# Modulation gathers inside the next step, and modulation rows behind the next step's weights

## The chip, the cores and the metric

The kernel runs on one core of one Trainium2 chip. The metric is the device time of one execution in microseconds (us), the median of several runs; lower is better. Engines are named as the profile names them: PE (TensorE, the matmuls), DVE (VectorE), ACT (ScalarE), POOL (GpSimd) and SP, whose queue issues the DMAs spoken of here.

## The reference, cut to what matters

Two layers of a trunk of width 1024 run over 640 tokens (512 of a sample, 128 of a prompt). Each layer is a feed-forward block (FFN1), a mixing block of attention and Fourier heads, and a second feed-forward block (FFN2). Nine modulation vectors of 1024 elements per layer and kind of token shift, scale and gate the three blocks; they come from a conditioning vector through the weight w_mod.

```python
def swiglu(h, w_gu, w_down):
    g, u = jnp.split(h @ w_gu, 2, axis=-1)
    return (jax.nn.silu(g) * u) @ w_down

    mod = jax.nn.silu(cvec) @ w_mod[l] + b_mod[l]
    sh1, sc1, gt1, sh2, sc2, gt2, sh3, sc3, gt3 = [m[:, None, :] for m in jnp.split(mod, N_MOD, -1)]
    f1 = swiglu(x * (1 + sc1) + sh1, w_ffn1_gu[l], w_ffn1_down[l])
    x = layer_norm(ALPHA * x + 0.5 * gt1 * f1, ln_g[l, 0], ln_b[l, 0])
    mo, new = token_mix(x * (1 + sc2) + sh2, ...)
    x = layer_norm(ALPHA * x + gt2 * mo, ln_g[l, 1], ln_b[l, 1])
    f2 = swiglu(x * (1 + sc3) + sh3, w_ffn2_gu[l], w_ffn2_down[l])
    x = layer_norm(ALPHA * x + 0.5 * gt3 * f2, ln_g[l, 2], ln_b[l, 2])
```

Inputs and weights are 32-bit floats. w_gu has 2 x 2816 columns, w_down 2816 rows.

## The kernel before

**Products.** Activations lie with the width on the partitions and the 640 tokens in two halves of 320 columns. Each 32-bit value is split in a high part (hi, ACT, L162) and the rest (lo, DVE, L167), so that a product of two values is three matmuls (L116 to L118), of 320 columns each.

**Weights.** A weight tile of 512 KB is a Unit. Its fetch (L146) loads it by SP's queue into a ring of four raw buffers; then ACT writes hi and DVE writes lo into rings of four, and the raw buffer is free again. A Pair (L184) loads two tiles at once and has a chain of sums on DVE between its raw buffers (L204 to L215); its matmuls are those of L121 to L123 (out of them pa, pb, pc, pd).

**A feed-forward block** has 22 tiles t of 128 hidden columns, in three parts of 8, 7 and 7. In FFN1 tiles t = 0 to 10 are plain: each is a step of a gate product g and an up product u, 96 matmuls in all, followed by silu and product (ACT L724, DVE L726) and the split of the result (L113). Tiles from 11 on are taken in pairs. After each part come eight down steps m = 0 to 7 (d, 48 matmuls in part 0), whose result DVE adds to the state xt with the gate (L985). In part 0 the down steps have DVE make the block sums for the pairs beside it (L751 to L757).

**Modulation.** A modulation vector is a group of eight rows of w_mod (each 128 x 1024). A row is a unit without hi and lo: it takes one raw buffer, and DVE multiplies it with the conditioning values into an accumulator of two halves (L368 for a group's first row, L370 for the other seven; two instructions for each row). After the eighth row a gather of four matmuls on PE (L380) adds over the partitions, ACT copies the result (L389), a turn of four transposes on PE (L395) puts it back on partitions, and DVE adds the bias (L400). There is one accumulator, so the first row of the next group waits for the gather of the last. FFN1 of each layer carries six groups (j = 2 to 7), FFN2 of layer 0 three, FFN2 of layer 1 one: 16 with a gather here.

**Order.** with_mods (L2002) puts rows behind the main steps: each main step adds its rate to a sum `due`, and for each whole one a row unit follows. The rates of FFN1 are 1.0 for t=0, 4.0 for t=1, 8/3 for the plain steps and 10/7; each down step of part 0 takes four. When a group's last row is placed, the list `late` gets the gather and the turn: the gather becomes a step of its own behind the next whole main step, and the turn one behind the step after that. The list `flat` of all units, in the order of the steps, is the order of loading, and so of SP's queue; prep_to loads and converts up to a step's units, and advance and fetch_ahead load and convert ahead as far as there is room in the rings (four raw buffers). A row unit that stands behind step t in the steps also stands ahead of the weights of step t+1 in that order. Within the steps the order of instructions on an engine is the scheduler's, which keeps to priorities of the program's order and to buffers.

Of the kernel before, what the change touches and what calls it, by code (L numbers as in the profile page):

```python
# [29 lines left out]
PARTS = (8, 7, 7)  # L30
MIDW = max(PARTS) * T
PLAIN = {1: 11, 2: 6}
MOD_RATE = {1: (1.0, 4.0, 8 / 3, 10 / 7), 2: (1.0, 3.0, 1.0, 8 / 6)}
BUSY = 2
T_BUFS = 9
E_BUFS = 6
# [23 lines left out]
def trunk_kernel(ctx: ExitStack, tc: tile.TileContext, a, y_prompt, y_sample, new_a_k, new_a_v, new_b_k, new_b_v):  # L60
# [171 lines left out]
        return Unit([(0, n, w[k0 * 128 : (k0 + nk) * 128, c0 : c0 + n].rearrange("(k p) c -> p k c", p=128))], nk, n)  # L232

    steps = []
    flat, index, ptr = [], {}, [0]

    def prep_to(n):
# [456 lines left out]
    def ffn_steps(l, which, gate_fn, pre=None):  # L694
# [150 lines left out]
        t = 0  # L845
        for pi, n in enumerate(PARTS):
            final = pi == len(PARTS) - 1
            for i in range(n):
                if t == 0:
                    u0, u1 = gu(0), gu(1)  # L850
                    u0[0].extra = True

                    def head(u0=u0, u1=u1):
                        if not pre:
                            new_mid()
                        with tc.manual_schedule() if pre else nullcontext():
                            if pre:
                                pre[0]()
                            accs = [Acc("g0", True), Acc("u0", False), Acc("g1", True)]
                            head_group([u0[0], u0[1], u1[0]], accs, pre and pre[1])  # L860
                        if pre:
                            new_mid()
                        finish(0, accs[0], accs[1])
                        loc["g1"] = accs[2]

                    steps.append(([u0[0], u0[1], u1[0]], head, bool(pre), 0.0 if pre else rates[0]))

                    def second(u1=u1):
                        pu = Acc("u1", False, bank)
                        for hf in range(2):  # L870
                            project(u1[1], pu.h[hf], hf)
                        finish(1, loc.pop("g1"), pu)
                        park(4)

                    step([u1[1]], second, rates[1])
                elif 1 < t < plain:
                    u = gu(t)

                    def body(u=u, i=i, t=t):
                        if i == 0:  # L880
                            new_mid()
                        pg, pu = Acc("g", True), Acc("u", False)
                        for hf in range(2):
                            project(u[0], pg.h[hf], hf)
                        for hf in range(2):
                            project(u[1], pu.h[hf], hf)
                        finish(i, pg, pu)
                        if t == 2:
                            park(4)
                        if which == 2:  # L890
                            for k in {3: (0, 1), 4: (2,), 5: (3,)}.get(t, ()):
                                block_sums(k)
                        if t == plain - 1:
                            block_third()

                    step(list(u), body, rates[2])
                elif t >= plain:
                    pair = Pair(cols(t * 128), cols(FFN + t * 128))
                    us = [pair, Sums(pair, "u"), Sums(pair, "g")]
                    loc[t] = us  # L900
                    pair.chained, pair.follows = i < n - 1, i > 0 and t > plain

                    def body(us=us, i=i, t=t, n=n):
                        if i == 0:
                            new_mid()
                        if i == 0 or t == plain:
                            loc["region"] = tc.manual_schedule(engines={ENG.PE, ENG.Activation, ENG.DVE})
                            loc["region"].__enter__()
                        seven(i, us, loc[t + 1] if i < n - 1 else None, t == FT - 1)
                        if i == n - 1:  # L910
                            loc.pop("region").__exit__(None, None, None)
                        if t == FT - 1:
                            unpark()

                    step(us, body)
                if i == n - 1 and not final:
                    last_gu = steps[-1]

                    def more(fn=last_gu[1]):
                        fn()  # L920
                        fetch(0)
                        fetch(1)

                    steps[-1] = (last_gu[0], more, *last_gu[2:])
                t += 1
# [9 lines left out]
            for m in range(KT - nskew):  # L935
                u = du(m)

                def body(u=u, m=m, n=n, pi=pi, final=final):
                    p = Acc("d", m % 2 == 0)
                    if final:  # L940
                        if m == 0:
                            ln.begin()
                        ln.pre(m)
                    for hf in range(2):
                        down_mm(u, p.h[hf], hf, n)
                    for hf in range(2):
                        if final:
                            ln.residual(m, hf, p.h[hf])
                        else:
                            plain_residual(xt[m], m, hf, p.h[hf], gate_fn())  # L950
                    if not final:
                        nc.sync.dma_start(out=parked[m], in_=xt.pop(m))
                        if m + 2 < KT:
                            fetch(m + 2)
                    if which == 1 and pi == 0 and m % 2 == 1:
                        block_sums(m // 2)

                step([u], body, 0.0 if final or m >= KT - BUSY + (which == 1) else rates[3])
# [1043 lines left out]
    def with_mods(build, mod_list):  # L2002
# [2 lines left out]
        main = steps[lo:]  # L2005
        del steps[lo:]
        groups = [mod_steps(*m) for m in mod_list]
        due, late = 0.0, []
        for s in main:
            steps.append(s)  # L2010
            while late:
                steps.append(([], late.pop(0), False, 0.0))
                if late:
                    break
            due += s[3]
            while groups and s[3] and due > 0.999:
                ms, gather, turn = groups[0]
                steps.append(ms.pop(0))
                due -= 1.0
                if not ms:  # L2020
                    groups.pop(0)
                    late += [gather, turn]
                    break
        assert not groups, len(groups)

    def fetch_late():
# [9 lines left out]
    for l in range(DEPTH):  # L2036
# [8 lines left out]
        with_mods(  # L2045
            lambda: ffn_steps(l, 2, gate_of(l, 8, True)), [(l, 8)] + ([(l + 1, 0), (l + 1, 1)] if l + 1 < DEPTH else [])
        )
    flat.extend(u for units, *_ in steps for u in units)
    index.update((id(u), i) for i, u in enumerate(flat))
    seen = 0  # L2050
    for units, fn, manual, _ in steps:
        seen += len(units)
        if not manual:
            prep_to(seen)
            if units and not getattr(units[0], "chained", False):
                advance()
            else:
                fetch_ahead()
# [66 lines left out]
```

## Time and profile before

| | |
|---|---|
| median of 3 runs | 2584.7 us (2583.87 to 2588.28) |
| the profiled execution | 2578.7 us |
| its span | 2576.9 us |
| granted PE clock, mean | 0.983 |
| PE busy | 96% of the span |
| DVE, ACT, POOL busy | 74%, 41%, 2% |
| DMA, read and written | 127 GB/s over the span |

[...] Idle time of an engine counts only where PE waits for it.

### The profile page before, as it was taken

To read this page: it belongs to the slowest core of one execution; us is meant where nothing else is said; L and a number is where in the kernel's file an instruction comes from. 1 tells how busy PE (TensorE), PEld (TensorE's weight loads), DVE (VectorE), ACT (ScalarE), POOL (GpSimd) and SP (SyncE) were. 2 spreads that over 40 slices of the span, in tenths; PEclk is the share of its full clock that TensorE was granted. 3 is DMA by queue.
4 is the path that set the end of the run, shared out by engine and by line. 5 is a ranking of instruction groups with operands and counts; after the bars stand their busy time and mean duration, and the time that the engine had idled before them with its cause. 6 is when DMAs were issued, how large, how long until landed. Compare 5 with 4: busy or idle time off the path is not lost. (4 is left out here: it accounts for less than half of the span.)

```text
span 2576.9 us, 41839 instructions
## 1 busy us (share of the span) xinstructions
PE 2467.0 (96%) x16759; PEld 2377.6 (92%) x16759; DVE 1916.2 (74%) x3266; ACT 1065.7 (41%) x1942; POOL 44.0 (2%) x42
## 2 busy tenths in 40 slices
PE   8889899999999999999998889999999999999998
PEld 6789899999879999999988889999998799999998
DVE  5568778776776896878784678787688678667577
ACT  3212324455675632424361123243666755323242
POOL 0000000001000000000000000000010000000000
PEclk9899999999999999999999899999999999999999
DMA  9556464423123445372444454624331225434332
GB/s 270 162 173 208 120 195 125 136 97 107 52 65 99 150 129 172 94 222 84 142 150 149 151 166 126 215 81 137 107 97 40 60 99 180 133 97 133 114 119 78
DMA packets 400560, 337.11 MB, mean 131 GB/s; under 512 B 13802, under 2 KB 352492, under 8 KB 399852
## 3 DMA queue, kind: packets, MB, share of 16 engines
q1 hardware_dynamic: 400364, 334.43, 42.4%
q8 instruction: 132, 2.16, 0.4%
q14 instruction: 64, 0.52, 0.1%
HBM read 286.93 MB, written 40.63 MB: 127 GB/s over the span
## 5 line engine op out<-in xcount | busy, mean ns | idle before, releaser
L162 ACT CAST hi<-raw 128x1024 fp32r<-128x1024 f32 (+5 forms) x382 | 388.0, 1018 | 805.5 <-PE pd L122 186.6
L167 DVE TENSOR_TENSOR lo<-raw,hi 128x1024 fp32r<-128x1024 f32 (+5 forms) x382 | 451.1, 1183 | 143.9 <-ACT hi L162 142.1
L116 PE MATMUL d<-midh,hi 128*128 128x320 f32 x1366 | 425.0, 312 | 14.2 <-ACT hi L162 14.2
L118 PE MATMUL d<-midh,lo 128*128 128x320 f32 x1366 | 423.6, 311 | 1.4 <-DVE lo L167 1.4
L117 PE MATMUL d<-midl,hi 128*128 128x320 f32 x1366 | 424.7, 311 | 0.1
L370 DVE SCALAR_TENSOR_TENSOR acc<-raw,csil,acc 128x1024 f32<-128x1024 f32 x224 | 277.7, 1277 | 7.4 <-DMA raw<-in_w_mod_dram 7.4
L116 PEld LDWEIGHTS d<-midh,hi 128*128 128x128 f32 x1366 | 258.1, 189 | 20.0 <-ACT hi L162 14.7
L117 PEld LDWEIGHTS d<-midl,hi 128*128 128x128 f32 x1366 | 258.4, 189 | 2.1 <-DVE midl L837 1.8
L118 PEld LDWEIGHTS d<-midh,lo 128*128 128x128 f32 x1366 | 257.9, 189 | 2.4 <-DVE lo L167 2.4
L116 PE MATMUL g<-hh,hi 128*128 128x320 f32 x480 | 154.4, 322 | 28.5 <-ACT hi L162 28.5
L118 PE MATMUL u<-hh,lo 128*128 128x320 f32 x544 | 168.2, 309 | 0.7 <-DVE lo L167 0.7
L116 PE MATMUL u<-hh,hi 128*128 128x320 f32 x544 | 168.3, 309 | 0.0
L117 PE MATMUL u<-hl,hi 128*128 128x320 f32 x544 | 168.3, 309 | 0.0
L118 PE MATMUL g<-hh,lo 128*128 128x320 f32 x480 | 153.8, 320 | 2.4 <-DVE lo L167 2.4
L117 PE MATMUL g<-hl,hi 128*128 128x320 f32 x480 | 153.5, 320 | 0.0
L985 DVE SCALAR_TENSOR_TENSOR xt<-d,gate,xt 128x320 f32<-128x320 f32 (+2 forms) x192 | 75.3, 433 | 91.3 <-PE d L118 91.1
L121 PE MATMUL pa<-hh,hi 128*128 128x320 f32 x432 | 134.4, 311 | 0.9 <-ACT up L797 0.7
L123 PE MATMUL pa<-hh,lo 128*128 128x320 f32 x432 | 133.6, 309 | 0.9 <-DVE lo L167 0.9
L122 PE MATMUL pa<-hl,hi 128*128 128x320 f32 x432 | 133.5, 309 | 0.0
L116 PEld LDWEIGHTS g<-hh,hi 128*128 128x128 f32 x480 | 94.6, 197 | 30.9 <-ACT hi L162 29.7
L118 PEld LDWEIGHTS u<-hh,lo 128*128 128x128 f32 x544 | 102.1, 188 | 1.0 <-DVE lo L167 1.0
L116 PEld LDWEIGHTS u<-hh,hi 128*128 128x128 f32 x544 | 102.1, 188 | 0.1
(608 smaller groups left out, 6353.1 us busy)
## 6 DMA issues: line engine op xcount, KB each, us to landing
raw<-in_w_ffn_gu_dram SPq DMA_DIRECT2D x176, 512.0 KB
raw<-in_w_mod_dram SPq DMA_DIRECT2D x128, 512.0 KB
raw<-in_w_ffn_down_dram SPq DMA_DIRECT2D x56, 448.0 KB
xt<-park SPq DMA_DIRECT2D x64, 320.0 KB
park<-xt SPq DMA_DIRECT2D x64, 320.0 KB
raw<-in_w_ffn_down_dram SPq DMA_DIRECT2D x36, 512.0 KB
raw<-in_w_in_dram SPq DMA_DIRECT2D x26, 512.0 KB
park<-trunk SPq DMA_DIRECT2D x32, 320.0 KB
```

What stands on the lines that cost most here:

```text
L116: nc.tensor.matmul(out, wh, xh, start=first, stop=False)
L117: nc.tensor.matmul(out, wh, xl, start=False, stop=False)
L118: nc.tensor.matmul(out, wl, xh, start=False, stop=last)
L121: nc.tensor.matmul(out, wh, xh, start=first, stop=False, skip_group_check=True)
L122: nc.tensor.matmul(out, wh, xl, start=False, stop=False, skip_group_check=True)
L123: nc.tensor.matmul(out, wl, xh, start=False, stop=last, skip_group_check=True)
L162: nc.scalar.copy(hi, self.raw.rearrange("p k n -> p (k n)"))
L167: nc.vector.tensor_sub(self.l, self.raw, self.h)
L370: nc.vector.scalar_tensor_tensor(acc[:, s, :], w, cs, acc[:, s, :], op0=ALU.mult, op1=ALU.add)
L985: nc.vector.scalar_tensor_tensor(x[:, s0:s1], ps[:, s0 - hf * HW : s1 - hf * HW], gate[:, m, s : s + 1], x[:, s0:s1], op0=ALU.mult, op1=AL ...
```

## The change

Three things are changed, all in the order of the work; no instruction is added or left out of what is computed.

The gather and the turn of a group no longer are steps. When the group's last row is placed, both are put on a list of hooks, and the next main steps call them from inside: a plain gate and up step calls one between the two halves of its up product and one after its end; a down step calls one after each half's product. The first gate and up steps and the pairs call none.

Row units no longer stand ahead of the next step's weights in the order of loading. They wait on a list, and follow the next units with a split; only a Pair has them ahead of it.

The rate of FFN1's plain steps is 3.0 where it was 8/3, and 0.0 in the last plain tile, t=10. Between t=2 and t=10 there are 24 rows either way.

```diff
--- before.py
+++ after.py
@@ -30,7 +30,7 @@
 PARTS = (8, 7, 7)
 MIDW = max(PARTS) * T
 PLAIN = {1: 11, 2: 6}
-MOD_RATE = {1: (1.0, 4.0, 8 / 3, 10 / 7), 2: (1.0, 3.0, 1.0, 8 / 6)}
+MOD_RATE = {1: (1.0, 4.0, 3.0, 10 / 7), 2: (1.0, 3.0, 1.0, 8 / 6)}
 BUSY = 2
 T_BUFS = 9
 E_BUFS = 6
@@ -232,6 +232,12 @@
         return Unit([(0, n, w[k0 * 128 : (k0 + nk) * 128, c0 : c0 + n].rearrange("(k p) c -> p k c", p=128))], nk, n)
 
     steps = []
+    hooks = []
+
+    def hook():
+        if hooks:
+            hooks.pop(0)()
+
     flat, index, ptr = [], {}, [0]
 
     def prep_to(n):
@@ -883,8 +889,11 @@
                         for hf in range(2):
                             project(u[0], pg.h[hf], hf)
                         for hf in range(2):
+                            if hf:
+                                hook()
                             project(u[1], pu.h[hf], hf)
                         finish(i, pg, pu)
+                        hook()
                         if t == 2:
                             park(4)
                         if which == 2:
@@ -893,7 +902,7 @@
                         if t == plain - 1:
                             block_third()
 
-                    step(list(u), body, rates[2])
+                    step(list(u), body, rates[2] if which == 2 or t < plain - 1 else 0.0)
                 elif t >= plain:
                     pair = Pair(cols(t * 128), cols(FFN + t * 128))
                     us = [pair, Sums(pair, "u"), Sums(pair, "g")]
@@ -943,6 +952,7 @@
                         ln.pre(m)
                     for hf in range(2):
                         down_mm(u, p.h[hf], hf, n)
+                        hook()
                     for hf in range(2):
                         if final:
                             ln.residual(m, hf, p.h[hf])
@@ -2005,22 +2015,25 @@
         main = steps[lo:]
         del steps[lo:]
         groups = [mod_steps(*m) for m in mod_list]
-        due, late = 0.0, []
+        due = 0.0
         for s in main:
             steps.append(s)
-            while late:
-                steps.append(([], late.pop(0), False, 0.0))
-                if late:
-                    break
             due += s[3]
             while groups and s[3] and due > 0.999:
                 ms, gather, turn = groups[0]
-                steps.append(ms.pop(0))
+                units, fn, *rest = ms.pop(0)
                 due -= 1.0
-                if not ms:
-                    groups.pop(0)
-                    late += [gather, turn]
-                    break
+                if ms:
+                    steps.append((units, fn, *rest))
+                    continue
+
+                def last(fn=fn, gather=gather, turn=turn):
+                    fn()
+                    hooks.extend([gather, turn])
+
+                steps.append((units, last, *rest))
+                groups.pop(0)
+                break
         assert not groups, len(groups)
 
     def fetch_late():
@@ -2045,13 +2058,18 @@
         with_mods(
             lambda: ffn_steps(l, 2, gate_of(l, 8, True)), [(l, 8)] + ([(l + 1, 0), (l + 1, 1)] if l + 1 < DEPTH else [])
         )
-    flat.extend(u for units, *_ in steps for u in units)
+    wait = []
+    for units, *_ in steps:
+        if units and not units[0].split:
+            wait += units
+        elif units:
+            flat.extend([*wait, *units] if isinstance(units[0], Pair) else [*units, *wait])
+            wait = []
     index.update((id(u), i) for i, u in enumerate(flat))
-    seen = 0
     for units, fn, manual, _ in steps:
-        seen += len(units)
+        if units and not manual:
+            prep_to(index[id(units[-1])] + 1)
         if not manual:
-            prep_to(seen)
             if units and not getattr(units[0], "chained", False):
                 advance()
             else:
```

The new listings number the lines from L372 on six higher (L368 is L374, L380 is L386) and those behind the down step's hook ten higher (L985 is L995).

**SP's queue, layer 0, around the weights of t=5.** Before; raw_878 and raw_884 are the weights of t=4, raw_1124 and raw_1130 those of t=5, raw_761 the last row of group 2, the four rows behind t=4 are the first of group 3, and the two cs loads belong to another table:

```order
L146 DMA raw_878<-in_w_ffn1_gu_dram 128x8x128
L146 DMA raw_884<-in_w_ffn1_gu_dram 128x8x128
L146 DMA raw_890<-in_w_mod_dram 128x1024
L146 DMA raw_894<-in_w_mod_dram 128x1024
L146 DMA raw_1003<-in_w_mod_dram 128x1024
L146 DMA raw_1007<-in_w_mod_dram 128x1024
L1920 DMA cs02_5286<-in_cache_b_k_dram 128x128
L1920 DMA cs03_5291<-in_cache_b_k_dram 128x128
L146 DMA raw_1124<-in_w_ffn1_gu_dram 128x8x128
L146 DMA raw_1130<-in_w_ffn1_gu_dram 128x8x128
```

After; raw_880 is a weight of t=4, raw_886 the last row of group 2, raw_890 and raw_894 are the weights of t=5, raw_898 to raw_1143 rows of group 3, and raw_1147 and raw_1153 the weights of t=6:

```order
L146 DMA raw_880<-in_w_ffn1_gu_dram 128x8x128
L146 DMA raw_886<-in_w_mod_dram 128x1024
L146 DMA raw_890<-in_w_ffn1_gu_dram 128x8x128
L146 DMA raw_894<-in_w_ffn1_gu_dram 128x8x128
L146 DMA raw_898<-in_w_mod_dram 128x1024
L146 DMA raw_1013<-in_w_mod_dram 128x1024
L146 DMA raw_1015<-in_w_mod_dram 128x1024
L146 DMA raw_1019<-in_w_mod_dram 128x1024
L146 DMA raw_1143<-in_w_mod_dram 128x1024
L146 DMA raw_1147<-in_w_ffn1_gu_dram 128x8x128
L146 DMA raw_1153<-in_w_ffn1_gu_dram 128x8x128
```

The weights of t=5 have moved from behind the first four rows of group 3 to ahead of all of them.

**DVE, layer 0, around the first row of group 3.** Before; acc0_2 and acc0_3 are the accumulator for groups 2 and 3, silu_1108 is t=4, and lo_1127 and lo_1133 belong to t=5:

```order
L726 TENSOR_TENSOR silu_1108<-silu_1108,u_0_1010 128x320
L726 TENSOR_TENSOR silu_1108<-silu_1108,u_1_1011 128x320
L368 TENSOR_SCALAR acc0_3_1121<-raw_890,csil_102 128x1024
L113 TENSOR_TENSOR midl_627<-silu_1108,midh_626 128x640
L368 TENSOR_SCALAR acc0_3_1121<-raw_890,csil_102 128x1024
L370 SCALAR_TENSOR_TENSOR acc0_3_1121<-raw_894,csil_102,acc0_3_1121 128x1024 x2
L370 SCALAR_TENSOR_TENSOR acc0_3_1121<-raw_1003,csil_102,acc0_3_1121 128x1024 x2
L167 TENSOR_TENSOR lo_1127<-raw_1124,hi_1126 128x1024
L370 SCALAR_TENSOR_TENSOR acc0_3_1121<-raw_1007,csil_102,acc0_3_1121 128x1024
L167 TENSOR_TENSOR lo_1133<-raw_1130,hi_1132 128x1024
```

After; silu_1127 is t=4, and lo_1006 and lo_1010 belong to t=5:

```order
L376 SCALAR_TENSOR_TENSOR acc0_2_734<-raw_757,csil_102,acc0_2_734 128x1024
L376 SCALAR_TENSOR_TENSOR acc0_2_734<-raw_886,csil_102,acc0_2_734 128x1024 x2
L167 TENSOR_TENSOR lo_1006<-raw_890,hi_1005 128x1024
L732 TENSOR_TENSOR silu_999<-silu_999,u_0_901 128x320
L732 TENSOR_TENSOR silu_999<-silu_999,u_1_902 128x320
L167 TENSOR_TENSOR lo_1010<-raw_894,hi_1009 128x1024
L113 TENSOR_TENSOR midl_631<-silu_999,midh_630 128x640
L374 TENSOR_SCALAR acc0_3_1140<-raw_898,csil_102 128x1024 x2
L732 TENSOR_TENSOR silu_1127<-silu_1127,u_0_1022 128x320
L376 SCALAR_TENSOR_TENSOR acc0_3_1140<-raw_1013,csil_102,acc0_3_1140 128x1024 x2
L732 TENSOR_TENSOR silu_1127<-silu_1127,u_1_1023 128x320
```

The two lo parts of t=5 have moved from behind the first row of group 3 to ahead of it.

**PE, layer 0, around the gather of group 5.** Before; u_1_2308 is the second half of t=8's up product and g_2429 the gate product of t=9:

```order
L116 MATMUL u_1_2308<-hh_116,hi_2173 128x320
L117 MATMUL u_1_2308<-hl_117,hi_2173 128x320
L118 MATMUL u_1_2308<-hh_116,lo_2174 128x320
L380 MATMUL ps_mod0_5_2411<-acc0_5_1868,ones_1_92 32x512 x4
L116 MATMUL g_2429<-hh_116,hi_2294 128x320
L117 MATMUL g_2429<-hl_117,hi_2294 128x320
L118 MATMUL g_2429<-hh_116,lo_2295 128x320
```

After; d_1_2116 is the second half of down step m=7 and g_2203 the gate product of t=8:

```order
L118 MATMUL d_1_2116<-midh_630,lo_1895 128x320
L116 MATMUL d_1_2116<-midh_630,hi_1894 128x320
L386 MATMUL ps_mod0_5_2141<-acc0_5_1807,ones_1_92 32x512 x2
L117 MATMUL d_1_2116<-midl_631,hi_1894 128x320
L118 MATMUL d_1_2116<-midh_630,lo_1895 128x320
L386 MATMUL ps_mod0_5_2141<-acc0_5_1807,ones_1_92 32x512 x2
L116 MATMUL g_2203<-hh_116,hi_1963 128x320
```

The gather has moved from behind t=8 into the last products of the down steps of part 0; that of group 4 stands in m=2, 264 matmuls ahead of it.

## Rows read from the trace of the kernel before

**Rows 1.** Page, part 1: busy us, share of the span, instructions of each engine.

```profile
PE 2467.0 (96%) x16759; PEld 2377.6 (92%) x16759; DVE 1916.2 (74%) x3266; ACT 1065.7 (41%) x1942; POOL 44.0 (2%) x42
```

**Rows 2.** Waits of PE: line waited for, us in total, times, longest us.

```profile
PE g L116 <- ACT hi L162: 28.5, 5, 8.1
PE d L116 <- ACT hi L162: 14.2, 2, 8.5
PE pb L121 <- ACT hi L162: 11.5, 2, 8.8
PE ps_modt L395 <- ACT mod_sb L389: 3.5, 4, 0.9
...
PE ps_mod L380 <- DVE acc L370: 0.5, 1, 0.5
```

**Rows 3.** Windows: us, then busy us (count) per engine, granted PE clock, DMA share, GB/s.

```profile
50.00:100.00 50.00, 45.25 (x294) 44.59 (x295) 34.69 (x40) 15.05 (x20) 0.00 (x0) 0.93 0.72 232
100.00:200.00 100.00, 85.70 (x546) 82.02 (x546) 60.78 (x82) 18.79 (x23) 0.00 (x0) 0.90 0.48 150
200.00:250.00 50.00, 50.00 (x344) 48.96 (x344) 43.06 (x63) 10.77 (x13) 0.00 (x0) 1.00 0.69 210
250.00:300.00 50.00, 39.80 (x254) 37.60 (x254) 38.20 (x50) 14.85 (x21) 0.00 (x0) 0.90 0.48 147
1300.00:1350.00 50.00, 45.57 (x286) 44.10 (x285) 44.44 (x69) 31.52 (x57) 0.00 (x0) 0.93 0.55 179
1350.00:1450.00 100.00, 80.97 (x518) 77.49 (x517) 51.38 (x60) 17.77 (x22) 0.00 (x0) 0.88 0.42 131
1500.00:1550.00 50.00, 42.92 (x274) 41.18 (x273) 35.60 (x50) 10.72 (x13) 0.00 (x0) 0.90 0.51 155
1550.00:1600.00 50.00, 46.60 (x305) 46.07 (x305) 42.13 (x56) 19.50 (x28) 0.00 (x0) 0.97 0.37 105
2200.00:2250.00 50.00, 50.00 (x343) 48.92 (x343) 30.82 (x49) 17.28 (x25) 0.00 (x0) 1.00 0.52 162
```

**Rows 4.** Windows of 5 us in the stall ahead of t=5, layer 0.

```profile
120.00:125.00 5.00, 1.29 (x3) 0.89 (x4) 4.62 (x5) 1.36 (x2) 0.00 (x0) 0.50 0.82 232
125.00:130.00 5.00, 5.00 (x22) 5.00 (x22) 4.99 (x8) 0.73 (x1) 0.00 (x0) 0.57 0.81 255
```

**Rows 5.** Timelines at that stall: start, us, engine line, out<-in, count [idle before <-releaser].

```profile
114.89 1.07 PE L380 MATMUL ps_mod<-acc,ones 128*32 128x512 f32 x8
...
116.02 0.75 DVE L368 TENSOR_SCALAR acc<-raw,csil 128x1024 f32<-128x1024 f32 x1 [0.54 <-PE ps_mod L380]
...
118.20 2.77 SPq L146 DMA_DIRECT2D raw<-in_w_ffn_gu_dram  x2
...
122.25 1.04 ACT L162 CAST hi<-raw 128x1024 fp32r<-128x1024 f32 x1 [5.48 <-DMA raw<-in_w_ffn_gu_dram]
...
123.35 0.63 PE L116 MATMUL g<-hh,hi 128*128 128x320 f32 x1 [6.26 <-ACT hi L162]
```

**Rows 6.** Timeline of SP's queue ahead of the first pair, layer 0.

```profile
270.47 5.85 SPq L146 DMA_DIRECT2D raw<-in_w_mod_dram  x3
278.39 18.49 SPq L184 DMA_DIRECT2D raw<-in_w_ffn_gu_dram  x6
```

**Rows 7.** Timeline of PE at the first pair, layer 1.

```profile
1564.87 0.42 PE L121 MATMUL pb<-t,hi 128*128 128x320 f32 x1 [2.71 <-ACT hi L162]
```

**Rows 8.** Window 187:226, down steps of part 0, layer 0; then DVE by line there.

```profile
187.00:226.00 39.00, 39.00 (x269) 37.96 (x268) 34.91 (x54) 7.58 (x10) 0.00 (x0) 1.00 0.70 226
...
L370 DVE SCALAR_TENSOR_TENSOR acc<-raw,csil,acc 128x1024 f32<-128x1024 f32 x10 | 12.2, 1276 | 0.0
L985 DVE SCALAR_TENSOR_TENSOR xt<-d,gate,xt 128x320 f32<-128x320 f32 (+2 forms) x16 | 6.4, 439 | 0.0
L167 DVE TENSOR_TENSOR lo<-raw,hi 128x1024 fp32r<-128x1024 f32 x5 | 6.1, 1225 | 4.8 <-ACT hi L162 4.8
L752 DVE TENSOR_TENSOR tg<-hh,hl 128x640 f32<-128x640 f32 x3 | 2.4, 816 | 0.0
```

## The prediction

> **What bounds the kernel now.** I read the page's busy shares first, then the waits of TensorE, then the span in stretches of 50 or 100 us, then the single instructions around one stall on all engines. PE is busy for 2467.0 us, 96% of the span [rows 1], so nothing but an idle or slowed PE can be won. The list of PE's waits puts most of its idle time on one releaser, ACT's conversion of a weight (L162): 28.5 us before gate products (g), 14.2 us before down products (d) and 11.5 us before pb, the second sum of a pair [rows 2]. That is 54.2 us in nine waits, and not the whole loss. In a stretch without a wait PE issues 343 to 344 matmuls in 50 us (200:250, 2200:2250), one each 50 / 343 = 0.1458 us; around the nine waits it issues fewer [rows 3]. 343 for each 50 us less the counts of the seven stretches that hold the nine waits gives 49, 138, 89, 57, 168, 69 and 38, in all 608 matmuls, at 0.1458 us 88.6 us. [...]
>
> What makes a stall, at 115 to 129 us [rows 5]: four modulation rows fill the ring of raw buffers. The first of them on DVE (L368, 116.02) writes the one accumulator and must wait until PE's gather of the last group (114.89) has read it. That gather is emitted after the whole of step t=4 and ahead of t=5. So the rows leave the ring only after it, SP issues t=5's weights at 118.20, ACT starts to convert at 122.25, and PE starts at 123.35, after 6.26 us of nothing. Five of the nine stalls have this form: t=5 and the first down step of part 0 in both layers, t=10 in layer 1. The other four come from the order of loading alone: rows of t=1 ahead of t=2's weights in both layers, and three rows of t=10 (270.47) ahead of the six loads of the first pair (278.39) in both [rows 6].
>
> **The change part by part.** *Gather inside the next step.* The four gather matmuls and four transposes are the same instructions as before, at another place, so they cost nothing of their own. The accumulator comes free in the middle of the next step. ACT's copy then has half a step of matmuls until the transposes, where PE waited 3.5 us in four places for that copy [rows 2]. One of those I found inside a stall already counted, so I count them at nothing; at best it is a further gain of 3.5.
>
> *Order of loading.* SP now issues t=5's two weights ahead of the first row that waits for the gather, and DVE makes both their lo parts ahead of it, as the listings of the order show. So the five gather stalls go: 138 + 168 + 69 = 375 matmuls, 54.7 us. In the other four the weights of t=2 and of the first pair no longer stand behind rows (a pair would keep waiting rows ahead of it, but t=10 has none any more): 49 + 89 + 57 + 38 = 233 matmuls, 34.0 us; t=1's own matmuls or t=10's hide the loads. What is late next is the load itself: from SP's issue at 118.20 to ACT's start at 122.25 are 4.05 us [rows 5], and a weight of the next step is now issued about a step of 96 x 0.1458 = 14.0 us ahead. So I leave nothing behind; the ends are 0 and 88.6 us, and I take the whole, since the order shows both causes gone at each place.
>
> *Rate.* 24 rows come in eight plain steps of three instead of nine of 8/3. DVE in such a step: three rows x 2 x 1.22 = 7.3 us, two lo parts x 1.22 = 2.4 (12.2 us for ten, 6.1 for five [rows 8]), and three short operations of silu and residue, each at most an L752 of 0.8, 2.4: 12.1 us beside 14.0 us of PE. It stays hidden, with 1.9 us to spare; without that cover it would cost what is lacking, up to 2.4 for each row more.
>
> *The new wait.* A gather that comes earlier also sets an earlier time by which DVE must be through with the group. The narrow place is the down steps of part 0, four rows a step: gather 4 now stands in m=2, gather 5 in m=7, and in PE's order 264 matmuls lie between, 264 x 0.1458 = 38.5 us (before, gather 5 had until the end of t=8). DVE's work in between: in 187:226 of the kernel before, 39 us, it was busy for 34.9 us, with 10 accumulating operations (L370), 5 lo parts, 16 residuals and block sums [rows 8]. In the new order there are 14, 6 and 15, and two whole blocks, without the one L752 and two operations of half its width that 187:226 has beside two blocks. That is 34.9 + 4 x 1.22 + 1.22 - 0.4 - (0.8 + 0.4 + 0.4) = 39.0 us. The first row starts 1.1 us after the gather (116.02 after 114.89 [rows 5]), so PE would wait 1.1 + 39.0 - 38.5 = 1.6 us if DVE never idled, and 5.7 if it kept the 4.1 us of idle time that it had in 187:226. A DVE that is behind finds its inputs ready, so I take about 2.7, nearer the lower end, and price it as the stall with that wait, the pair of layer 1: 2.71 us of wait, 38 matmuls, 5.5 us lost [rows 3, 7]. In both layers that is 11 us; the ends are 0 and 2 x 10 (the stall at t=10 of layer 1, 69 matmuls, 10.1 us). Behind the waiting gather on PE are the last products of m=7 and then t=8; ACT's copy and DVE's turn wait for it.
>
> The 4.05 us of a load are part of DVE's idle time there. [...]
>
> **Sum.** The profiled execution took 2578.7 us (span 2576.9). 2578.7 - 88.6 + 11 = 2501.1. The median of the runs is 2584.7, 6.0 more, so I say 2507. The case's own range: new waits hidden and the 3.5 us won, 2584.7 - 92.1 = 2493; new waits at 20 and one stall of 7 left, 2584.7 - 88.6 + 27 = 2523.
>
> **Rivals.** A: *only the gather stalls go.* The other four are bound by the transfers, not by their order: in 50:100 the DMA engines move 232 GB/s at a share of 0.72 [rows 3], and a pair needs six loads with a chain of DVE sums before pb can start. Then 34.0 us stay: 2584.7 - 54.7 + 11 = 2541. Against it: the six loads could not be issued until 278.39, after the three rows [rows 6], and the FFN2 parts, with the same pairs and few rows, show no wait of this kind (2200:2250 [rows 3]).
>
> B: *slower; PE waits at each gather.* The gather comes half a step or more earlier, rows compete with the lo parts of two steps, and DVE is behind everywhere; PE, which issues its products in order, stands in the middle of a step. If each of the 16 gathers cost what the stall at t=2 costs (49 matmuls, 7.1 us [rows 3]), that is 113.6 us against 88.6 won: 2584.7 + 25.0 = 2610. It decides from 88.6 / 16 = 5.5 us per gather. For it: the narrow place above is of this kind. Against it: only one gather of 16 waited for DVE before, for 0.5 us [rows 2], and most of them keep more than a step of slack. [...]
>
> C: *the stall only moves by one step.* The rows still fill the ring and still wait for a gather, so not the next weights but those after them come late, and nothing is won: 2585. Against it: in the new order at most one step's rows stand between two steps' weights, and the gather that they wait for comes half a step before those loads must be issued.
>
> **How the numbers follow.** Forecast 0.76, A 0.14, B 0.05, C 0.05. The forecast alone does not hold 0.8, so the range reaches over A and below the case's low end: 2490 to 2545. About 0.2% (5 us) is what a measurement of this kernel can tell from no change. Faster by more: 0.90 (forecast and A); within it: 0.05 (C); slower: 0.05 (B).
>
> **What would show it.** Right: the waits of PE on L162 before g, d and pb fall from 54.2 us to under 5; each of the seven stretches has some 343 matmuls per 50 us at clock 1.00; SP issues t=5's weights ahead of the rows; a wait of ps_mod on DVE's acc of 1 to 5 us stands near m=7 of part 0 in both layers, and no other. Wrong: waits on L162 stay at t=2 and at the first pair (A); ps_mod waits in many groups (B); the waits on L162 stand one step later (C); or the clock falls below 1.00 in places where none of the nine stood.

## The result and the profile after

The median fell from 2584.64 us (2583.87 to 2588.28, 4 runs) to 2512.05 us (2511.24 to 2516.32, 4 runs); the ratio is 0.972, 95% interval 0.9703 to 0.9737. The forecast was 2507 with a range of 2490 to 2545. The profiled execution of the changed kernel took 2516.32 us (span 2514.5, clock 0.995) and is the longest of its four (the other spans are 2508.7 to 2509.7), while that of before was below the others of its kernel; so the two traces lie 62.4 us apart and the medians 72.6.

The page's first part (columns as in [rows 1]): PE's busy time fell by 13.9 us for the same matmuls, at a mean granted clock of 0.995 where it was 0.983, and its share rose to 98%.

```profile
PE 2453.1 (98%) x16759; PEld 2361.8 (94%) x16759; DVE 1914.3 (76%) x3266; ACT 1066.2 (42%) x1942; POOL 43.9 (2%) x42
```

PE's waits, the answers to [rows 2] (us in total, times, longest):

```profile
PE ps_mod L386 <- DVE acc L376: 11.8, 2, 7.3
...
PE d L116 <- ACT midh L112: 2.7, 2, 1.4
...
PE ps_modt L401 <- ACT mod_sb L395: 2.1, 1, 2.1
```

No wait of g, d or pb on ACT L162 is left; there were 54.2 us in nine. In their place stand two waits of the gather for DVE, 11.8 us, one of a turn for its copy, and two of a down product for midh.

The stretches of [rows 3] again, and 1450:1500 besides, since layer 1 now comes some 30 us earlier (columns as there):

```profile
50.00:100.00 50.00, 50.00 (x347) 49.65 (x340) 38.90 (x47) 18.29 (x24) 0.00 (x0) 1.00 0.82 257
100.00:200.00 100.00, 98.30 (x662) 93.27 (x661) 80.88 (x110) 21.86 (x27) 0.00 (x0) 1.00 0.67 205
200.00:250.00 50.00, 45.50 (x291) 41.59 (x290) 44.34 (x60) 12.76 (x16) 0.00 (x0) 0.93 0.62 195
250.00:300.00 50.00, 50.00 (x343) 50.00 (x343) 37.12 (x59) 19.35 (x27) 0.00 (x0) 1.00 0.25 72
1300.00:1350.00 50.00, 47.95 (x317) 46.65 (x316) 39.65 (x44) 12.74 (x15) 0.00 (x0) 0.97 0.75 223
1350.00:1450.00 100.00, 96.94 (x660) 94.08 (x658) 76.16 (x102) 21.04 (x26) 0.00 (x0) 1.00 0.66 201
1450.00:1500.00 50.00, 44.26 (x282) 40.68 (x283) 41.60 (x58) 13.37 (x17) 0.00 (x0) 0.93 0.56 168
1500.00:1550.00 50.00, 50.00 (x343) 50.00 (x342) 39.82 (x57) 20.84 (x31) 0.00 (x0) 1.00 0.31 90
1550.00:1600.00 50.00, 50.00 (x342) 48.73 (x341) 40.78 (x58) 11.26 (x14) 0.00 (x0) 1.00 0.75 245
```

Of the 608 matmuls that were missing, 343 for each 50 us less the counts now gives 24 (100:200), 52 (200:250), 26 (1300:1350), 26 (1350:1450) and 61 (1450:1500), 189 in all or 27.6 us. 88.6 - 27.6 = 61.0 us, nearly all of the 62.4 us between the two traces. So the stretches tell where the time came from, and where the rest stayed. DVE, SP and ACT at t=4 and t=5 of layer 0, the answers to [rows 5]:

```profile
105.80 1.42 DVE L374 TENSOR_SCALAR acc<-raw,csil 128x1024 f32<-128x1024 f32 x2 [8.70 <-PE ps_mod L386]
...
110.03 4.04 SPq L146 DMA_DIRECT2D raw<-in_w_ffn_gu_dram  x2
...
114.99 1.05 ACT L162 CAST hi<-raw 128x1024 fp32r<-128x1024 f32 x1 [3.77 <-DMA raw<-in_w_ffn_gu_dram]
```

The first row of group 3 still waits for the gather, and DVE is idle for 8.70 us before it. But t=5's lo parts lie behind that wait no more, and the loads at 110.03 are t=6's, a whole step early. The same wait costs PE nothing here: in each 5 us of 100:125 it was busy throughout, with 35 to 38 matmuls at a granted clock of 1.00.

The two new waits (timeline of PE, start, us, idle before) and DVE's work ahead of the first, between the gathers 4 and 5 of layer 0 (a window with the columns of [rows 3], then DVE by line, count, busy us and idle us, the answers to [rows 8]):

```profile
219.98 1.07 PE L386 MATMUL ps_mod<-acc,ones 128*32 128x512 f32 x2 [4.50 <-DVE acc L376]
...
1455.74 1.07 PE L386 MATMUL ps_mod<-acc,ones 128*32 128x512 f32 x2 [7.29 <-DVE acc L376]
```

```profile
176.40:219.90 43.50, 39.08 (x268) 38.81 (x266) 38.06 (x55) 9.06 (x11) 0.00 (x0) 0.97 0.69 210
...
L376 DVE SCALAR_TENSOR_TENSOR acc<-raw,csil,acc 128x1024 f32<-128x1024 f32 x14 | 17.5, 1276 | 0.0
L167 DVE TENSOR_TENSOR lo<-raw,hi 128x1024 fp32r<-128x1024 f32 x6 | 7.3, 1225 | 5.4 <-ACT hi L162 5.2
L995 DVE SCALAR_TENSOR_TENSOR xt<-d,gate,xt 128x320 f32<-128x320 f32 (+2 forms) x15 | 6.0, 432 | 0.0
```

The counts are those of the forecast, 14, 6 and 15, and DVE's busy time of 38.06 us is near the 39.0 that it had added up. DVE's idle time is what was misjudged: it stayed at 5.4 us before lo parts, for weights whose hi part came late, and 1.2 us before the first row. One of these weights, from SP's issue to ACT's start, and DVE's lo parts between the two gathers of layer 1 (window 1403:1455.7):

```profile
184.49 0.38 SPq L146 DMA_DIRECT2D raw<-in_w_ffn_down_dram  x1
190.20 1.05 ACT L162 CAST hi<-raw 128x1024 fp32r<-128x1024 f32 x1 [9.38 <-DMA raw<-in_w_ffn_down_dram]
...
L167 DVE TENSOR_TENSOR lo<-raw,hi 128x1024 fp32r<-128x1024 f32 x7 | 8.6, 1224 | 8.2 <-ACT hi L162 8.2
```

This load took 5.7 us to ACT's start, where the forecast had 4.05. Layer 1 is not like layer 0, as the forecast took it to be: its t=0 carries a row, which that of layer 0 does not, so gather 4 stands one down step earlier, in m=1. Between its gathers 4 and 5 DVE has 14, 7 and 17 operations and a third block of sums, beside more matmuls on PE, and it idled 8.2 us before lo parts.

The third new wait, in layer 1: ACT's timeline, PE's turn and the stretch behind it:

```profile
1328.05 1.04 ACT L162 CAST hi<-raw 128x1024 fp32r<-128x1024 f32 x1 [8.94 <-DMA raw<-in_w_ffn_gu_dram]
1329.00 0.58 ACT L395 COPY mod_sb<-ps_mod 128x512 f32<-128x512 f32 x1
...
1322.67 1.20 PE L386 MATMUL ps_mod<-acc,ones 128*32 128x512 f32 x8
...
1329.63 0.55 PE L401 MATMUL ps_modt<-ident,mod_sb 128*128 128x128 f32 x3 [2.05 <-ACT mod_sb L395]
...
1320.00:1330.00 10.00, 7.95 (x54) 6.65 (x53) 4.54 (x7) 1.95 (x3) 0.00 (x0) 1.00 0.47 150
1330.00:1340.00 10.00, 10.00 (x60) 10.00 (x59) 9.45 (x13) 2.67 (x4) 0.00 (x0) 0.83 0.70 203
```

The gather ended at 1323.9 (1322.67 + 1.20), but on ACT the copy of its result stands behind a conversion that waited 8.94 us for its load. The turn waited 2.05 us for it, and the next stretch ran at a granted clock of 0.83: the 20 us of both rows hold 54 + 60 = 114 matmuls of 137, which is 3.4 us lost.

The fourth, at the first down step of part 0, in both layers:

```profile
159.34 0.56 PE L116 MATMUL d<-midh,hi 128*128 128x320 f32 x2 [1.34 <-ACT midh L112]
...
155.00:165.00 10.00, 8.60 (x57) 8.07 (x56) 8.68 (x10) 2.83 (x3) 0.00 (x0) 1.00 0.90 275
```

The down product needs t=7's result, which goes over DVE and ACT. Before, a gather and a longer wait stood here and covered it. 57 matmuls of 69 in 10 us: 1.7 us, the clock at 1.00.

### The profile page after: what moved, and what is told of

Same layout as the page of the kernel before. It is cut to its first block, busy times and chain, and to the rows that moved or that the text cites. A ratio compares the mean times of both kernels' runs of the same rounds, so it can differ in the third digit from the quotient of the medians.

```text
span 2514.5 us, 41842 instructions
## 1 busy us (share of the span) xinstructions
PE 2453.1 (98%) x16759; PEld 2361.8 (94%) x16759; DVE 1914.3 (76%) x3266; ACT 1066.2 (42%) x1942; POOL 43.9 (2%) x42
## 5 line engine op out<-in xcount | busy, mean ns | idle before, releaser
L162 ACT CAST hi<-raw 128x1024 fp32r<-128x1024 f32 (+5 forms) x382 | 388.5, 1018 | 771.4 <-PE d L117 197.3
L167 DVE TENSOR_TENSOR lo<-raw,hi 128x1024 fp32r<-128x1024 f32 (+5 forms) x382 | 451.4, 1183 | 143.0 <-ACT hi L162 141.0
L995 DVE SCALAR_TENSOR_TENSOR xt<-d,gate,xt 128x320 f32<-128x320 f32 (+2 forms) x192 | 75.7, 433 | 82.6 <-PE d L118 82.5
L117 PEld LDWEIGHTS u<-hl,hi 128*128 128x128 f32 x544 | 102.1, 188 | 0.1
```

The source lines that it names most:

```text
L117: nc.tensor.matmul(out, wh, xl, start=False, stop=False)
L162: nc.scalar.copy(hi, self.raw.rearrange("p k n -> p (k n)"))
L167: nc.vector.tensor_sub(self.l, self.raw, self.h)
L995: nc.vector.scalar_tensor_tensor(x[:, s0:s1], ps[:, s0 - hf * HW : s1 - hf * HW], gate[:, m, s : s + 1], x[:, s0:s1], op0=ALU.mult, op1=AL ...
```

## The experiments

The theory: rows of the next group fill the raw ring and wait for the gather, and the next weights stand behind them; the order of loading cures that, with the rate for the first pair. The rivals: the gather's earlier place does it, or the transfers as such are too slow (A of the forecast). All runs stand against the kernel before on the same chip, whose medians there were 2584.85 (first four), 2582.13 (next four) and 2580.53 us (last three).

**The order of loading alone**

```diff
-    flat.extend(u for units, *_ in steps for u in units)
+    wait = []
+    for units, *_ in steps:
+        if units and not units[0].split:
+            wait += units
+        elif units:
+            flat.extend([*wait, *units] if isinstance(units[0], Pair) else [*units, *wait])
+            wait = []
...
-            prep_to(seen)
+            prep_to(index[id(units[-1])] + 1)
```

> The kernel before with one part of the change: row units follow the next step's weights in the order of loading. Gathers stay steps of their own, the rate stays 8/3. Theory (the order of loading is what cures the stalls of t=2 and of the gathers; the pair keeps its rows of t=9 and t=10 ahead of it): PE's waits on L162 before g nearly vanish, those before pb stay; of 88.6 us some 70 are won, less up to 20 if the first down step of part 0 still stands behind its rows: 2515 to 2535 us. Rival (the gather inside the step is what frees the ring, the order alone only moves the wait by one step): within 10 us of 2585.

Measured: 2537.58 us, ratio 0.9815 (0.9801 to 0.983), 47.3 us won. PE's waits:

```profile
PE pb L121 <- ACT hi L162: 16.7, 2, 9.2
PE ps_mod L380 <- DVE acc L370: 5.8, 3, 2.9
...
PE d L116 <- ACT hi L162: 2.2, 1, 2.2
...
PE g L116 <- ACT hi L162: 1.3, 2, 1.1
```

28.5 us before g are 1.3, 14.2 before d are 2.2. So the order cures the gather stalls and t=2 without the gather being moved. The pairs wait 16.7 us where they waited 11.5: in this order the rows of t=9 and of t=10, six in layer 0 and seven in layer 1, stand ahead of their loads. The total is 2.6 us above the stated range: the expectation left out that the pairs would wait longer, and 5.8 us of waits of gathers for DVE. Two of these three are gather 4's, in the down steps of part 0 of both layers.

**The hooks alone** (the list and the three hook calls, as in the change; order and rate as before)

> The kernel before with one part of the change: gather and turn run inside the next main step. Order of loading and rate as before. Theory: the accumulator comes free half a step (3.5 us) earlier, but the next weights still stand behind the waiting rows; each of the five gather stalls shrinks by 3.5 to 5 us and none vanishes, the other four stay, and the new wait of gather 5 adds up to 16: 2560 to 2583 us. Rival (the gather's place is what matters): the five vanish, 2584.6 - 54.7 + 16 = 2546 us or less.

Measured: 2560.93 us, ratio 0.9909 (0.9892 to 0.9925), 23.9 us won.

```profile
PE g L116 <- ACT hi L162: 17.6, 5, 5.3
PE pb L121 <- ACT hi L162: 13.6, 2, 8.8
PE d L116 <- ACT hi L162: 7.9, 2, 5.3
```

All nine waits are still there, the longest of g 5.3 where it was 8.1 us. A gather 24 matmuls earlier shortens each of the five gather stalls, by 2.7 to 4.7 us of wait, and removes none, as the theory had it; the other four are not shorter in sum (pb 13.6 us where it was 11.5). The added wait of gather 5 did not come: no wait of ps_mod for DVE is in the list. With the old rate group 5's last row stands behind t=8, so its gather runs in t=9 (at 256.44 us in layer 0), with or without hooks.

**The rate alone**

```diff
-MOD_RATE = {1: (1.0, 4.0, 8 / 3, 10 / 7), 2: (1.0, 3.0, 1.0, 8 / 6)}
+MOD_RATE = {1: (1.0, 4.0, 3.0, 10 / 7), 2: (1.0, 3.0, 1.0, 8 / 6)}
...
-                    step(list(u), body, rates[2])
+                    step(list(u), body, rates[2] if which == 2 or t < plain - 1 else 0.0)
```

> The kernel before with one part of the change: three rows in each plain step of FFN1 and none in t=10. Theory (the two pair stalls come from t=10's rows ahead of the pair's loads): PE's wait before pb vanishes in both layers, 18.5 us, and in layer 1 the gather stall at t=10, 10.1 us, may go with its rows: 2556 to 2568 us; the stalls at t=2, t=5 and the first down step stay. Rival (the pair's six loads and sums are themselves too slow): no gain, 2585.

Measured: 2543.78 us, ratio 0.9838 (0.9822 to 0.9853), 41.1 us won, 12 more than the best that was expected.

```profile
PE g L116 <- ACT hi L162: 26.1, 4, 8.7
PE d L116 <- ACT hi L162: 4.7, 2, 3.3
...
PE ps_mod L380 <- DVE acc L370: 2.5, 3, 1.1
...
1300.00:1350.00 50.00, 45.07 (x288) 44.14 (x287) 40.57 (x61) 27.70 (x49) 0.00 (x0) 0.93 0.60 189
1350.00:1400.00 50.00, 50.00 (x344) 48.96 (x343) 31.01 (x35) 11.68 (x14) 0.00 (x0) 1.00 0.50 148
1400.00:1450.00 50.00, 42.13 (x267) 39.37 (x266) 39.89 (x49) 10.51 (x13) 0.00 (x0) 0.90 0.65 203
1500.00:1550.00 50.00, 50.00 (x344) 49.99 (x344) 41.32 (x55) 20.63 (x27) 0.00 (x0) 1.00 0.51 147
```

The waits before pb are gone (no line has them), and so is the stall at t=10 of layer 1 (1500:1550). What the expectation missed is that the rate also moves the ends of the groups: in layer 1 the stretch 1350:1400 is whole (344), where before it held the stall at t=5, and only 1300:1350 (t=2) and 1400:1450 (now t=7) are left. The two waits before d are not at the first down step either, but at two later ones of layer 0.

**Order and hooks, the old rate**

> The changed kernel without its change of rate: rows at 8/3 in t=2 to t=10. Theory: since a pair takes the waiting rows ahead of it, six rows stand ahead of the first pair and the pair stalls come back, 18.5 us or more: 2528 to 2540. Rival (order and hooks do all): within 5 us of 2512.

Measured: 2520.46 us, ratio 0.9751 (0.9737 to 0.9766).

```profile
PE pb L121 <- ACT hi L162: 12.0, 2, 7.1
PE ps_mod L386 <- DVE acc L376: 5.4, 3, 3.4
```

The pairs keep 12.0 us of waits, as expected. The 5.4 us of waits for DVE are gather 4's, in the down steps; the 11.8 with the new rate are gather 5's, which the old rate leaves in t=9. So the rate takes the pairs' wait away and brings a longer wait of a gather. The total is 7.5 us better than the range, which did not subtract that part. Alone, the three parts give 47.3 + 23.9 + 41.1 = 112.3 us and together 72.6: each takes something off the same stalls.

**Order and rate, without hooks**

> The changed kernel without its hooks: gather and turn are steps of their own as before, the order of loading and the rate are the new ones. Theory (the order of loading and the rows gone from t=10 cure the stalls; the half step by which a gather comes earlier is worth little on top): 2512 to 2525 us, with the wait of gather 5 still there, since its rows end at the same place. Rival (the hooks are worth on top what they are worth alone, 23.9 us): 2536 us or more, with waits on L162 back before g or d.

Measured: 2514.28 us, ratio 0.9733 (0.9719 to 0.9748).

```profile
PE ps_mod L380 <- DVE acc L370: 15.3, 3, 8.1
```

Within the measurement this is the changed kernel (0.972, 0.9703 to 0.9737), with not one wait on L162 before g, d or pb. The waits of gathers for DVE are there without any hook, and longer. So it isn't the hook that brings them, as the forecast had it ("a gather that comes earlier"). Order alone has 5.8 us of them, the rate alone 2.5, both 15.3, of which 8.15 and 5.78 are gather 5's. With three rows in each plain step group 5's last row stands behind m=6 and no longer behind t=8, so its gather comes at m=7, as a step or by a hook, and the weights, no longer late themselves, don't give DVE time.

**The gather of group 5 later** (in the middle of t=8's up product, 74 matmuls or 10.8 us further on)

```diff
                         down_mm(u, p.h[hf], hf, n)
-                        hook()
+                        if which == 2 or pi or m < KT - 1:
+                            hook()
```

> The changed kernel, but the last down step (m=7) of part 0 in FFN1 calls no hook, so that gather 5 runs in the middle of t=8, half a step to a whole one later. Theory (the waits of gather 5 on DVE, 4.5 and 7.3 us, and the slow clock behind them, 52 and 61 matmuls missing in their stretches, are the price of a gather that comes before DVE is through): both vanish, some 16 us: 2496 us, between 2493 and 2502. Rival (DVE's lateness passes on to the lo parts of the next steps): no gain, 2508 to 2515.

Measured: 2495.51 us, ratio 0.9666 (0.9651 to 0.968); once more, later, 2495.90 us, ratio 0.9669 (0.9655 to 0.9683).

> The kernel with the late gather 5 once more, beside the last two on one chip: 2495 us, within 3, whatever the theory; it is the base for their difference.

DVE's timeline with the last row of group 5, and PE's gather, layer 0:

```profile
218.03 1.28 DVE L376 SCALAR_TENSOR_TENSOR acc<-raw,csil,acc 128x1024 f32<-128x1024 f32 x1
...
225.82 1.07 PE L386 MATMUL ps_mod<-acc,ones 128*32 128x512 f32 x8
```

The last operation of the row ends at 220.5, the gather comes at 225.82 and waits for nothing. The two stretches with the waits had lacked 52 + 61 = 113 matmuls, 16.5 us. The median, too, is 16.5 us below the changed kernel's, but beside that one the kernel before took 2584.64 us and here 2582.13. Against the kernel before on the same chip this one wins 86.6 us, and 84.6 in the repeat, where the changed kernel won 72.6: a gain of 12.0 to 14.0 us. Within the intervals that agrees with 16.5; that the two figures are equal is chance. DVE's lateness is not passed on: the rival falls. This is the fastest kernel of the study.

**The gather that reads no accumulator, in the kernel before**

```diff
-                nc.tensor.matmul(ps[32 * g : 32 * g + 32, :], ones_1, acc[:, g // 2, ...], ...)
+                for q in range(4):
+                    nc.tensor.matmul(ps[32 * g : 32 * g + 32, 128 * q : 128 * q + 128], ones_1, ident, ...)
```

> The kernel before, but the gather multiplies a constant tile in place of the accumulator (so the modulation it makes is not the reference's; the same PE time in 16 matmuls of 128 columns). The first row of a group then has no gather to wait for. Theory (one accumulator holds the rows in the ring): the five gather stalls vanish, 54.7 us, and the four at t=2 and the first pair stay: 2530 us, waits on L162 before pb still 11 us. Rival (the rows ahead in SP's queue and DVE's work on them make the weights late, the accumulator does not matter): 2575 us or more.

Measured: 2529.56 us, ratio 0.979 (0.9773 to 0.9808). The number met the expectation for a wrong reason. The 16 small matmuls take longer than the four: 2.46 us for 32 records (the one at 104.48 below), against 1.07 us for 8 [rows 5], so 16 gathers cost some 16 x 1.39 = 22.2 us more, which the expectation put at nothing. Without them 2529.56 - 22.2 = 2507, 74.8 us below its kernel before. The five gather stalls are 54.7 of that; the pairs' 89 + 38 = 127 matmuls, 18.5 us, would be nearly all of the rest. This is an estimate: new waits, the longest of them the 5.5 us before d below, are not taken off. The waits:

```profile
PE g L116 <- ACT hi L162: 6.9, 2, 4.9
PE d L116 <- ACT midh L112: 5.5, 1, 5.5
```

Indeed only the two at t=2 are left before g, and none before pb. So the stalls of the pairs, too, hang on the accumulator: the rows ahead of the pair's loads wait for gather 5, which in the kernel before came at the end of t=9. The forecast had put them under "the order of loading alone".

**The same free gather in the changed kernel**

> The changed kernel with the same free gather (the modulation that it makes is not the reference's). No gather waits for DVE and no row for a gather. Theory: the two waits of gather 5 vanish with their slow clock, 16 us, and the late copy ahead of layer 1's first turn may go too, 3 us: 2493 to 2497 us. Rival (DVE behind in the down steps holds back lo parts all the same): 2505 us or more, with waits of d or g on L167.

Measured: 2523.38 us, ratio 0.9766 (0.975 to 0.9783). PE at the gather of group 2, and a wait further on:

```profile
104.48 2.46 PE L387 MATMUL ps_mod<-ident,ones 128*32 128x128 f32 x32
...
133.63 0.35 PE L337 MATMUL ps_v<-ident,vrows 51*128 51x51 f32 x1 [7.13 <-DVE vec L320]
```

The total decides nothing: it holds the 22.2 us of the longer gathers and a wait of 7.13 us (granted clock 0.90 in its stretch, 100:150) of a transpose for a copy on DVE (L320) that stands elsewhere in this kernel's order. Less 22.2 us it is 2501. What it does show: no wait for DVE's acc, and none of d or g for a lo part on L167, against the rival.

**No hooks, gather 5 a step later**

```diff
-                    late += [gather, turn]
+                    late += [gather, turn] if len(groups) != 2 or len(mod_list) != 6 else [lambda: None, gather, turn]
```

> New order of loading and new rate, gather and turn as steps of their own (no hooks), and the gather of group 5 of FFN1 one main step later, behind t=8. It asks what the hooks are worth once the wait of gather 5 is out of the way. Theory (the order of loading and the rate did the cure, the half step matters little): 2495 to 2503 us, within 8 us of the kernel with hooks and the late gather 5 (2495.5). Rival (without the half step the rows free the ring too late): waits on L162 before g or d come back, 2510 us or more.

Measured: 2500.91 us, ratio 0.9689 (0.9676 to 0.9702), beside 2495.90 and 0.9669 (0.9655 to 0.9683) with hooks on the same chip.

```profile
PE u L116 <- DVE xt L985: 5.2, 1, 5.2
```

No wait on L162 comes back. Some 5 us remain for the hooks at most, and the intervals just overlap. PE's longest wait left here is that of t=8's up product for DVE's residual of a down step of part 0: the place is the narrow one, whichever product meets it.

**The copy on DVE**

```diff
-            nc.scalar.copy(box["sb"], ps)
+            nc.vector.tensor_copy(box["sb"], ps)
```

> The kernel with the late gather 5, and the gather's result copied by DVE in place of ACT. In the changed kernel the copy stood on ACT behind a conversion that waited 8.9 us for its load, and PE waited 2.05 us for it before layer 1's first turn (2.1 us in two places with the late gather 5). Theory (the copy stands behind a late conversion in ACT's order): these waits vanish, 2 to 5 us: 2490 to 2494 us. Rival (DVE's 16 copies of about 0.6 us and what they push back cost as much): within 2 us of 2495.5, or above.

Measured: 2504.59 us, ratio 0.9702 (0.9689 to 0.9716), 8.7 us slower than the same kernel with the copy on ACT. PE's waits for the copy, and DVE at the longer of them:

```profile
PE ps_modt L401 <- DVE mod_sb L395: 4.7, 2, 3.3
...
235.84 1.23 DVE L167 TENSOR_TENSOR lo<-raw,hi 128x1024 fp32r<-128x1024 f32 x1 [3.60 <-ACT hi L162]
236.98 0.69 DVE L395 COPY mod_sb<-ps_mod 128x512 f32<-128x512 f32 x1
```

The theory fell. Turns wait for the copy 4.7 us in two places. In the one shown, at the end of t=8, the copy (0.69 us) stands in DVE's order behind a lo part that waited 3.60 us for its hi part: it is behind a late conversion again, now through DVE. The rest of the 8.7 us was not traced.

## Why the prediction was right

**Right.** *The nine stalls.* All waits on L162 before g, d and pb are gone, and the order listing had shown it: each weight ahead of the first row that waits. The term of 88.6 us holds, but for 2.8 us that are left below without a cause. The 34.4 us of it beyond the 54.2 us of waits lie in stretches with a granted clock under 1.00 [rows 3]; in [rows 4] the one at 0.57 has no idle time and 22 matmuls in 5 us, where 36 came at 1.00 (75:80 before). *The rate* stays hidden in the plain steps: in 50:100, with t=2 and t=3, PE has 347 matmuls. *The place of the new wait*, m=7 of part 0 in both layers and nowhere else. *DVE's work* there in layer 0, 14, 6 and 15 operations. A, that only the gather stalls go, did not come: the first pairs and t=2 run through. B, a wait at each gather, came at 2 of 16. C, that the stalls move on by a step, has no trace. Not all signs came as they were named: layer 1's new wait is 7.29 us and not 1 to 5, and one sign of being wrong did come, a clock of 0.83 behind layer 1's first turn, where none of the nine stalls stood.

**Off in size: the new wait.** Forecast 2 x 2.7 us, priced at 11 us by the stall of layer 1's first pair, behind which the granted clock was 0.66 (1565:1570 before). Measured 4.50 and 7.29 us, with 0.56 in 220:225 and 0.50 in 1455:1460, and 113 matmuls, 16.5 us. The failed step is "a DVE that is behind finds its inputs ready", by which the lower end was taken: DVE idled 5.4 us for hi parts in layer 0, more than the 4.1 of the upper end, which gave 5.7 us, and 8.2 us in layer 1, which was not counted by itself. The code issues a load when DVE has freed a raw buffer, so a late DVE should get its next input late as well. SP's waits in 176.4:219.9 bear it out, 11.5 us for DVE's row operations and 7.7 us for its lo parts, but no run tested it by itself. The idle time that the trace had shown should have been kept in the sum. The experiment with the later gather shows the price to be 12.0 to 16.5 us.

**Wrong in its account, without effect on the sum: the pairs.** They were said to stall by the order of loading alone. With the order alone they stall longer (16.7 us), and with a gather that reads no accumulator not at all; the rate's zero in t=10 is what freed them. And gather 5's wait comes by the order and the rate, not by the hook: the rate moves group 5's last row from t=8 to m=6, and without hooks the wait is there all the same, 8.15 and 5.78 us.

**Errors in the text up to the forecast.** The down steps of part 0 take 10/7 rows each, the fourth figure of MOD_RATE, and m=7 none; not four. The rate of 1.0 for t=0 holds in layer 1 alone. The hook between the halves of the up product stands behind 72 of a step's 96 matmuls, so ACT's copy has 24 matmuls, 3.5 us, until the turn and not half a step. And in the listing of PE around gather 5, u_1_2308 is t=9 and g_2429 is t=10, so that group 5 had until the end of t=9, not t=8. The count of rows between the gathers and the 264 matmuls were read from the order of layer 0, so the sum made for it doesn't change.

**Not foreseen:** the turn behind a late conversion on ACT (3.4 us) and midh at the first down step (1.7 and 1.8 us). With 16.5 in place of 11 they explain 12.4 of the 15.2 us by which the profiled execution (2516.3) lies above the sum of 2501.1 made for it. In the medians 5 us of it are left, because the 6.0 us added for the distance between the profiled execution and the median went the other way: the profiled execution of after lies 4.3 us above its median. That part of the agreement is luck.

## What to carry to other kernels

A resource with one buffer (here the accumulator) stalled what was queued behind its first writer, 54.7 us in five places, so put the next step's loads and conversions ahead of that instruction in every queue: its wait then cost PE nothing even where it was longer, as the 8.70 us here. When a consumer is moved forward, add up what its producer engine must do by then, idle time for its own inputs included, and leave a step of slack: here 74 matmuls later for one gather of a layer was worth 12.0 to 16.5 us in all. Parts of a change that cure the same stall don't add up; test them alone and together.

## What the runs showed of the hardware

Behind some waits the granted clock fell, and more time was lost than the wait. In the changed kernel waits of 1.34 and 1.40 us before the first down step left it at 1.00 (155:165, 1390:1400) and cost 1.7 and 1.8 us; one of 2.05 us was followed by 0.66 in 1330:1335 and cost 3.4 us, and one of 4.50 us by 0.56 in 220:225 and cost 7.6 us (52 matmuls). The length of a wait alone did not say whether the clock fell: in the repeat of the kernel with the late gather 5 a wait of 1.43 us before the first down step was followed by 0.66 in 160:165 (0.97 over 150:200), and with order and hooks, at the old rate, one of 3.36 us before a gather (184.04) left it at 1.00 (150:200).

The gather's four matmuls of 512 columns took 1.07 us [rows 5], and sixteen of 128 columns with the same output 2.46 us (104.48 in the changed kernel with the free gather).

PE kept to its order while it waited: before gather 5 of layer 0 in the changed kernel it was idle for 4.50 us, though the down product's two matmuls behind the gather read tiles that matmuls at 215.17 and before had read already.
